# First feed-forward product of a hybrid decoder block as seven half-size products

## The chip, the cores and the metric

The kernel runs on one core of one Trainium2 chip. The metric is device time in microseconds (us) of one execution, the median of three runs. The engines that matter here are TensorE (PE in the profile, with its weight loads as PEld), VectorE (DVE), ScalarE (ACT), GpSimd (POOL) and SyncE (SP); SP, ACT and POOL can also issue transfers.

## The reference

One decoder layer on 512 tokens of width 1024, all float32. A gated mixer (a pooling branch and an attention branch) is added to x; then comes the feed-forward part, which is what the change is about; then a last norm.

```
x   = x + (gate_a * a + gate_b * bm) @ w_out
hm  = rmsnorm(x, g_mlp)
x   = x + square(relu(hm @ w_mlp_in)) @ w_mlp_out     # w_mlp_in 1024 x 4096, w_mlp_out 4096 x 1024
out = rmsnorm(x, g_final)
```

## The kernel before

**Precision.** Each matmul operand is split in two float32r parts, hi (a rounding copy on ScalarE, L62) and lo (the rest, a subtraction on VectorE, L63). A product is three matmuls: hi·hi, hi·lo and lo·hi (`mm3`, L67 to L69, for products with the weights as stationary operand; `rows_mm`, L762 to L764, for those with the rows as stationary operand).

**Weights.** `load_chunk` (L93) loads 512 KB of a weight matrix into a `raw` tile (four buffers), issued by SP, and `split` makes `whi` and `wlo` (four buffers each). The second feed-forward product's pairs (`pair_of`, L841) use the same four `whi`/`wlo` buffers.

**Stages.** In order: first norm, latents, pooling and the gate A product (to about 142 us), eight attention heads with the gate B product filling in (to 260 us), attention projection, `w_out` product with the second norm and its transposes (to 350 us), then the feed-forward part. Before the feed-forward loop an order written out by hand (`manual_schedule`) holds in the first stage and around the `w_out` product. Elsewhere a planner orders each engine's instructions ahead of time by priority and its own cost model, and may move a ready instruction ahead of one that is not.

**Feed-forward part.** The 4096 hidden columns are four groups (`q` = 0 to 3) of eight blocks of 128. For each block, `load_up` loads and splits 1024 x 128 of `w_mlp_in`, `up_mm` makes 24 matmuls (8 slices of the contraction, 3 passes) of 128 x 512 into one PSUM bank, and `up_end` (L854) applies relu and square on ScalarE. The first three blocks run as two token halves each (256 columns), because the last rows' norm is not done yet (L816 to L823). When both blocks of a pair are done, `up_end` forms the sums S1, S3, S2, S4 of the hidden values' quarters and splits seven forms of them into `rhi`/`rlo`.

`down(q)` (L908) then makes the second product of the group by seven products of half-size quarters (a Winograd form). Its weight sums are formed in SBUF by adding transfers that GpSimd issues (`plus`, L922) onto `X` tiles, of which there are six buffers. Each product takes 168 / 7 = 24 matmuls of 128 x 512, in two banks. Results are added by VectorE (L906) into the residual rows `xa` or into U, V5 and V7, which `flush` (L1029) adds up before the last group.

Of the kernel before, what the change touches and what calls it, by code (L numbers as in the profile page):

```python
# [11 lines left out]
F32 = mybir.dt.float32  # L12
F32R = mybir.dt.float32r
I32 = mybir.dt.int32
AF = mybir.ActivationFunctionType
# [26 lines left out]
NX = 6  # L42
# [3 lines left out]
def block_kernel(ctx: ExitStack, tc: tile.TileContext, x, positions, g_mix, w_in, b_gate,  # L46
# [46 lines left out]
    def load_chunk(srcs, cols, parts=False, own=None):  # L93
# [3 lines left out]
        raw = wp.tile([P, 1024], F32, name=f"raw{n}", tag="raw", bufs=4)  # L97
        hi = (own or wp).tile([P, 1024], F32R, name=f"whi{n}", tag="whi", bufs=3 if own else 4)
        lo = (own or wp).tile([P, 1024], F32R, name=f"wlo{n}", tag="wlo", bufs=3 if own else 4)
# [63 lines left out]
    gB = spill.tile([P, KD, S], F32, name="gB")  # L163

# [65 lines left out]
    with ExitStack() as pre:  # L230
# [334 lines left out]
        pool_in(1)  # L565
        latents_t(3)
        pool_diff(0)
        load_u(3)
        pool_in(2)
        pool_diff(1)  # L570
        load_a(0)
        split(praw, pw_hi, pw_lo)
        pool_in(3)
        q_rotary_w()
        load_a(1)
        gate_a(0)
        pool_diff(2)
# [3 lines left out]
        gate_a(1)  # L581
        pool_diff(3)
# [3 lines left out]
        gate_a(2)  # L586
        load_p(0)
# [5 lines left out]
        gate_a(3)  # L593
        pool_proj(0)
# [3 lines left out]
        gate_a(4)  # L598
        pool_proj(2)
        load_a(6)  # L600
        gate_a(5)
        pool_proj(3)
        load_p(2)
        load_a(7)
        gate_a(6)
        project_w(0)
# [13 lines left out]
    with ExitStack() as att:  # L620
# [82 lines left out]
        for h in range(NH):  # L703
            if h + 1 < NH:
                project_w(h + 1)
            scores(h, 0)
            scores(h, 1)
# [21 lines left out]
    m_hi = keep.tile([P, KD, S], F32R, name="m_hi")  # L729
    m_lo = keep.tile([P, KD, S], F32R, name="m_lo")  # L730
    g2 = keep.tile([P, D], F32, name="g2", tag="g")
# [35 lines left out]
    w1_v = w_mlp_in.rearrange("(k p) c -> p k c", p=P)  # L767
    w2_v = w_mlp_out.rearrange("(k p) c -> p k c", p=P)
    nc.sync.dma_start(g2, g_mlp.partition_broadcast(P))
    wp2 = pool(norm, "wp2")  # L770
    order = ExitStack()
    order.enter_context(tc.manual_schedule(engines=ENGINES))
    hrow, wo, up_w = {}, {}, {}
# [3 lines left out]


    NG = FF // P // FFG
    HALF = FFG // 2  # L780
    ff_order = [q * FFG + j + k * HALF for q in range(NG) for j in range(HALF) for k in range(2)]

    def load_up(ff, own=None):
        up_w[ff] = chunk(w1_v[:, :, ff * P:(ff + 1) * P], KD, P, own=own)

    for k2 in range(4):
        load_out(0, k2)
    for c in range(2):
        cs = slice(c * 512, (c + 1) * 512)
        for t in range(NT):  # L790
# [10 lines left out]
            if c == 1:  # L801
                if t:
                    transpose_rows(hrow[t - 1], t - 1, m_hi, m_lo, psT, "n2")
                hrow[t] = norm_rows(xa[:, t, :], t, g2, tmp, "n2")
                if t < 3:
                    load_up(ff_order[t], own=wp2)
# [5 lines left out]
    def up_mm(w, ps, tok):  # L812
        proj_t(ps[:, tok], w, m_hi[:, :, tok], m_lo[:, :, tok], 0, KD, KD)


    lo_t, hi_t = slice(0, 256), slice(256, 512)  # L816
    first = [(up_w.pop(f), psM.tile([P, S], F32, name=f"up{f}", tag="mm")) for f in ff_order[:3]]
    up_mm(*first[0], lo_t)
    up_mm(*first[1], lo_t)
    transpose_rows(hrow[3], 3, m_hi, m_lo, psT, "n2")  # L820
    up_mm(*first[2], lo_t)
    for f in range(3):
        up_mm(*first[f], hi_t)  # L823
# [12 lines left out]
    A21, A11, S3, S1, S2, S4, A22, A12 = range(8)  # L836
# [4 lines left out]
    def pair_of(raw):  # L841
# [5 lines left out]
        return [t.rearrange("p (a b) -> p a b", a=2) for t in (hi, lo)]  # L847

    U, V5, V7 = (fp.tile([P, 2, 512], F32, name=n) for n in ("U", "V5", "V7"))
    C = {(1, c): xa[:, 2:4, c * 512:(c + 1) * 512] for c in range(2)}  # L850
    C.update({(2, c): xa[:, 0:2, c * 512:(c + 1) * 512] for c in range(2)})
    forms, F_of = {}, {}

    def up_end(ff, ps):  # L854

        q, j, k = ff // FFG, ff % FFG % HALF, ff % FFG // HALF
        if k == 0:
            F_of[q, j] = fp.tile([P, 8, 256], F32, name=f"F{q}_{j}", tag="F", bufs=1)
# [17 lines left out]
    for n in range(3):  # L876
        up_end(ff_order[n], first[n][1])
# [201 lines left out]
```

## Time and profile before

| | before |
|---|---|
| median of three runs | 700.42 us (700.18 to 700.74) |
| the profiled execution | 699.11 us |
| its span, first to last instruction | 697.3 us |
| mean granted TensorE clock | 0.992 |
| VectorE, ScalarE, GpSimd busy | 433.5, 325.7, 82.3 us |
| transfers | 93.07 MB, 133 GB/s over the span |

Times below are microseconds from the start of the span. In the groups of instructions a row names line, engine, operation, tiles (out<-in) and shape, then the busy time in us and the mean duration in ns of one, then the engine's idle time just before them and who ended it. Matmul durations there overlap each other; the distance between two starts says what one costs.

### The profile page before, as it was taken

How to read it: one execution, taken by the hardware profiler on the slowest of the kernel's cores; microseconds unless marked ns; L12 is line 12 of the kernel's file. 1: busy time of each engine (PE TensorE's matmuls, PEld its weight loads, DVE VectorE, ACT ScalarE, POOL GpSimd, SP SyncE). 2: the span in 40 equal slices, each digit the busy share in tenths (PEclk: the TensorE clock that was granted, in tenths of full speed). 3: DMA queues.
4: the chain of work that ended last, by engine and by line, in shares of the span. 5: the costliest groups of instructions: out<-in, count | busy, mean ns of one | idle time of the engine just before them, and what ended most of it. 6: DMA issues, size and time to landing. Idle time of an engine off the chain costs nothing.

```text
span 697.3 us, 8522 instructions
## 1 busy us (share of the span) xinstructions
PE 681.9 (98%) x3177; PEld 558.8 (80%) x3177; DVE 433.5 (62%) x693; ACT 325.7 (47%) x509; POOL 82.3 (12%) x98
## 2 busy tenths in 40 slices
PE   6999999999999999999999999999999999999994
PEld 3988888888888888888898888887888888888883
DVE  5868642678878745534655556346764467945776
ACT  4545332556556445312534653455434553355534
POOL 2317400000000000000002021001210102101111
PEclk8999999999999999999999999999999999999998
DMA  7424343542301227644467679535994458903453
GB/s 269 137 62 126 92 150 110 164 120 68 101 23 50 88 89 245 183 134 132 125 181 239 137 167 230 163 71 112 185 238 119 92 120 205 244 3 60 97 85 121
DMA packets 101314, 93.07 MB, mean 133 GB/s; under 512 B 6404, under 2 KB 75800, under 8 KB 101272
## 3 DMA queue, kind: packets, MB, share of 16 engines
q1 hardware_dynamic: 92568, 75.74, 35.1%
q0 software_dynamic: 8704, 16.78, 14.9%
q8 instruction: 25, 0.41, 0.2%
q14 instruction: 17, 0.14, 0.1%
HBM read 86.22 MB, written 6.29 MB: 133 GB/s over the span
## 4 chain that ended last, share of the span: by engine, by line
PE 93%; DVE 2%; DMA 2%; ACT 1%; issue 1%; SPq 0%; POOL 0%; POOLq 0%; DVEq 0%; ACTq 0%
PE up L69 9%; PE up L67 9%; PE up L68 9%; PE P L763 7%; PE P L764 7%; PE P L762 7%; PE u L406 3%; PE lat L338 3%; PE wo L764 2%; PE ga L68 2%; PE wo L762 2%; PE ga L69 2%; PE wo L763 2%; PE ga L67 2%; PE bm L69 2%; PE bm L67 2%
## 5 line engine op out<-in xcount | busy, mean ns | idle before, releaser
L63 DVE TENSOR_TENSOR wlo<-raw,whi 128x1024 fp32r<-128x1024 f32 x73 | 89.4, 1230 | 64.2 <-ACT whi L62 58.7
L62 ACT CAST whi<-raw 128x1024 fp32r<-128x1024 f32 x73 | 75.9, 1050 | 101.5 <-PE up L68 32.8
L67 PE MATMUL up<-m_hi,whi 128*128 128x512 f32 (+1 forms) x280 | 105.5, 377 | 0.0
L69 PE MATMUL up<-m_hi,wlo 128*128 128x512 f32 (+1 forms) x280 | 105.3, 376 | 0.0
L68 PE MATMUL up<-m_lo,whi 128*128 128x512 f32 (+1 forms) x280 | 105.3, 376 | 0.0
L63 DVE TENSOR_TENSOR xlo<-X,xhi 128x1024 fp32r<-128x1024 f32 x56 | 68.3, 1223 | 50.3 <-ACT xhi L62 50.2
L62 ACT CAST xhi<-X 128x1024 fp32r<-128x1024 f32 x56 | 58.5, 1049 | 73.0 <-PE P L764 56.3
L763 PE MATMUL P<-xlo,rhi 128*128 128x512 f32 (+1 forms) x228 | 88.5, 391 | 0.0
L762 PE MATMUL P<-xhi,rhi 128*128 128x512 f32 (+1 forms) x228 | 88.5, 391 | 0.0
L764 PE MATMUL P<-xhi,rlo 128*128 128x512 f32 (+1 forms) x228 | 87.7, 391 | 0.0
L924 POOL DMA_DIRECT2D X<-in_w_mlp_out x32 | 38.4, 1205 | 276.4 <-DVE xlo L63 215.3
L68 PEld LDWEIGHTS up<-m_lo,whi 128*128 128x128 f32 x280 | 52.7, 188 | 10.5
L69 PEld LDWEIGHTS up<-m_hi,wlo 128*128 128x128 f32 x280 | 52.6, 188 | 10.5
L67 PEld LDWEIGHTS up<-m_hi,whi 128*128 128x128 f32 x280 | 52.6, 188 | 10.5
L762 PEld LDWEIGHTS P<-xhi,rhi 128*128 128x128 f32 x228 | 42.8, 188 | 10.5
L764 PEld LDWEIGHTS P<-xhi,rlo 128*128 128x128 f32 x228 | 42.7, 188 | 10.1
L763 PEld LDWEIGHTS P<-xlo,rhi 128*128 128x128 f32 x228 | 42.8, 188 | 9.9
L63 DVE TENSOR_TENSOR rlo<-F,rhi 128x1792 fp32r<-128x1792 f32 x16 | 32.4, 2026 | 21.7 <-ACT rhi L62 21.7
L62 ACT CAST rhi<-F 128x1792 fp32r<-128x1792 f32 x16 | 27.0, 1689 | 19.7 <-DVE F L870 19.7
L861 ACT ACTIVATE F<-up 128x512 f32<-128x512 f32 x32 | 18.9, 594 | 21.0 <-DVE rlo L63 13.5
L67 PE MATMUL gb<-h_hi,whi 128*128 128x512 f32 x64 | 26.4, 412 | 0.0
L650 ACT ACTIVATE p<-s,nm 128x128 f32<-128x128 f32 (+3 forms) x32 | 16.8, 527 | 19.7 <-DVE nm L647 19.0
(236 smaller groups left out, 1314.9 us busy)
## 6 DMA issues: line engine op xcount, KB each, us to landing
raw<-in_w_mlp_in SPq DMA_DIRECT2D x32, 512.0 KB, 4.9
X<-in_w_mlp_out SPq DMA_DIRECT2D x32, 512.0 KB, 5.0
X<-in_w_mlp_out POOLq DMA_DIRECT2D x32, 512.0 KB, 6.1
raw<-in_w_in SPq DMA_DIRECT2D x20, 512.0 KB, 3.9
raw<-in_w_attn_proj SPq DMA_DIRECT2D x8, 512.0 KB, 3.6
raw<-in_w_out SPq DMA_DIRECT2D x8, 512.0 KB, 4.1
x<-in_x SPq DMA_DIRECT2D x4, 512.0 KB, 8.4
raw<-in_w_pool_proj SPq DMA_DIRECT2D x4, 512.0 KB, 3.3
```

The costliest lines, as they stand in the source:

```text
L62: nc.scalar.copy(hi, src)
L63: (lo_eng or nc.vector).tensor_tensor(out=lo, in0=src, in1=f32(hi), op=ALU.subtract)
L67: nc.tensor.matmul(acc, whi, ahi, start=first, stop=False)
L68: nc.tensor.matmul(acc, whi, alo, start=False, stop=False)
L69: nc.tensor.matmul(acc, wlo, ahi, start=False, stop=last)
L338: nc.tensor.matmul(ps[:, :LAT], h[:, k, tok], w[:, k % 2, :], start=len(done) == 1, stop=len(done) == 3 * KD)
L406: nc.tensor.matmul(ps, w[:, k, :], a[:, k, :], start=n + k == 0, stop=n == 2 and k == KD - 1)
L762: nc.tensor.matmul(acc, a_hi, w_hi, start=first, stop=False, skip_group_check=again)
L763: nc.tensor.matmul(acc, a_hi, w_lo, start=False, stop=False, skip_group_check=again)
L764: nc.tensor.matmul(acc, a_lo, w_hi, start=False, stop=last, skip_group_check=again)
L861: nc.scalar.activation(a, ps, AF.Relu)
L924: nc.gpsimd.dma_start(X[name, h].rearrange("p (a b) -> p a b", a=2), B[src, h], accum_op=ALU.add)
```

## The change

**The first product.** Each group `q` is now done in two passes (`d` = 0, 1) of 2 x 256 hidden columns. The contraction (1024) is cut in halves, the hidden columns of a group in halves, and the tokens in halves. With B the quarters of the transposed normed rows, and A those of the weights, a pass `up(q, d)` makes seven products: A11·B11, S1·T1, S2·T2, A12·B21, S3·T3, S4·B22 and A22·T4. S1 to S4 are sums of weight quarters, T1 to T4 sums of row quarters. Each product is 24 matmuls of 256 columns into one PSUM bank (`up_mm`: 2 blocks, 4 slices, 3 passes). The partial sums are shared in PSUM: ScalarE copies a bank once its first product is in (b from a, c from b, v from c), and later products go on adding to the copy and to the original.

**The weight sums.** In DRAM, ten sums of 1 MB (S1, S3, S2, S4 for group 0, S1 and S3 for groups 1 to 3) are formed early: a copy of one quarter, issued by ScalarE, in the first stage (`sum_copies`), and later an adding transfer of another quarter, issued by GpSimd (`sum_adds`: two in the first stage, one in each attention head). S2 and S4 of groups 1 to 3 are formed in SBUF: once S1's `raw` tile has been split, an adding transfer of 512 KB turns it into S2, and after S2's split another turns it into S4.

**What goes with it.** The four row sums T1 to T4 are formed and split once, right after the second norm. The rows' transposes are kept in float32 as well (`mT`, a ScalarE copy of each). The six `X` buffers of the second product are now one `X` buffer and the four `raw` ones, shared with the weights of the first; A11 of groups 1 to 3 uses the `X` buffer too. V7 is gone: that product is added to two rows' quarters at once. `gf` (the last gain) is loaded before the last `down` and not ahead of the loop. The seven forms of the second product's input are made per pass, for two blocks at a time.

```
+    IN_DRAM = [(q, n) for q in range(NG) for n in ((1, 3, 2, 4) if q == 0 else (1, 3))]
+    sums = {(q, n): spill.tile([P, 4, HALF * P], F32, name=f"S{n}_{q}") for q, n in IN_DRAM}
+    def sum_copies():
+        for q, n in IN_DRAM:
+            nc.scalar.dma_start(sums[q, n], block(q, {1: "21", 3: "11", 2: "11", 4: "12"}[n]))
+            yield
+    def sum_adds():
+        for q, n in IN_DRAM:
+            src = block(q, "22") if n == 1 else block(q, "21") if n == 3 else sums[q, 1 if n == 2 else 2]
+            nc.gpsimd.dma_start(sums[q, n], src, accum_op=ALU.add, max_dma_last_dim=2048)
+            yield
...
         pool_in(0)
+        next(copies)
...
             scores(h, 0)
+            next(adds)
...
+    def load_form(q, d, name, own=None):
...
+        if n in sums or not n:
+            src = (sums[n] if n else block(q, name[1:]))[:, :, cols]
+            raw = fp.tile([P, 1024], F32, name=f"XA{q}_{d}", tag="X", bufs=1) if q and name == "A11" else None
...
+                raw, hi, lo = load_chunk([(v, src)], 1024, True, own=own)
+        else:
+            raw = chain[q, d]
+            nc.gpsimd.dma_start(v(raw), block(q, {"S2": "11", "S4": "12"}[name])[:, :, cols], accum_op=ALU.add)
...
+    def transpose_norm(t):
+        for half in range(2):
...
+            if name != "B12":
+                hi, lo = (v[:, :, t % 2 * P:(t % 2 + 1) * P] for v in M[name])
+                split(pt, hi, lo)
+            nc.scalar.copy(mT[:, ks, tok], pt)
...
+    def up_mm(q, d, name, form, acc, fresh=False):
+        whi, wlo = up_w.pop((q, d, name))
+        bhi, blo = M[form]
+        for j in range(2):
+            js = slice(j * P, (j + 1) * P)
+            for k in range(4):
+                for n, (w, b) in enumerate(((whi, bhi), (whi, blo), (wlo, bhi))):
+                    nc.tensor.matmul(acc[:, j, :], w[:, k, js], b[:, k, :], start=fresh and j + k + n == 0,
+                                     stop=j == 1 and k == 3 and n == 2, skip_group_check=not fresh)
+    def start_up(q, d, ps=psM, tag="mm"):
+        a = bank(f"a{q}_{d}", ps, tag)
+        up_mm(q, d, "A11", "B11", a, fresh=True)
+        b = bank(f"b{q}_{d}")
+        nc.scalar.copy(b, a)
+        return a, b
+    ab = [start_up(0, 0), start_up(0, 1)]
+    transpose_norm(3)
+    for d in range(2):
+        up_mm(0, d, "A12", "B21", ab[d][0])
...
+    nc.vector.tensor_sub(tf[0], B["B11"], B["B12"])
+    split(tf[0], *M["T1"])
+    nc.vector.scalar_tensor_tensor(out=tf[1], in0=tf[0], scalar=-1.0, in1=B["B22"], op0=ALU.mult, op1=ALU.subtract)
+    split(tf[1], *M["T2"])
...
+    def up(q, d):
...
+        need("S1")
+        e = bank(f"e{q}_{d}", psU, "up")
+        up_mm(q, d, "S1", "T1", e, fresh=True)
+        e_sb = F[:, S1]
+        nc.scalar.copy(e_sb, e)
+        need("S2")
+        up_mm(q, d, "S2", "T2", b)
+        c = bank(f"c{q}_{d}")
+        nc.scalar.copy(c, b)
+        if q:
+            need("A12")
+            up_mm(q, d, "A12", "B21", a)
+        relu2(A21, a)
+        need("S3")
+        up_mm(q, d, "S3", "T3", c)
+        v = bank(f"d{q}_{d}")
+        nc.scalar.copy(v, c)
+        need("S4")
+        up_mm(q, d, "S4", "B22", b)
+        nc.vector.tensor_add(F[:, A12], e_sb, c)
+        nc.vector.tensor_add(F[:, A11], e_sb, b)
+        relu2(A12, F[:, A12], -1.0)
+        relu2(A11, F[:, A11])
+        pairs(A11, A11 + 1)
+        need("A22")
+        up_mm(q, d, "A22", "T4", v)
+        relu2(A22, v, -1.0)
+        flat = F.rearrange("p f j c -> p f (j c)")
+        nc.vector.tensor_sub(flat[:, S1], flat[:, A21], flat[:, A22])
+        nc.vector.tensor_tensor(out=flat[:, S3:S2 + 1:2], in0=flat[:, 0:S1 + 1:3],
+                                in1=flat[:, A11].unsqueeze(1).to_broadcast([P, 2, 512]), op=ALU.subtract)
+        nc.vector.tensor_add(flat[:, S4], flat[:, A12], flat[:, S2])
+        pairs(S3, S2 + 1)
+        pairs(S4, S4 + 1)
+        pairs(A22, A12 + 1)
...
-                X[name, h] = fp.tile([P, 1024], F32, name=f"X{name}_{q}_{h}", tag="X", bufs=NX)
+                own = (name, h) == ("11", 0)
+                X[name, h] = (fp if own else wp).tile([P, 1024], F32, name=f"X{name}_{q}_{h}",
+                                                      tag="X" if own else "raw", bufs=1 if own else NRAW)
...
-        if last:
-            into(C[2, 1], p7)
-            into(C[2, 0], p7, ALU.subtract)
-        else:
-            set_or_add(V7, p7)
+        into(C[2, 1], p7)
+        into(C[2, 0], p7, ALU.subtract)
...
     for q in range(NG):
-        for ff in ff_order[max(q * FFG, 3):(q + 1) * FFG]:
-            load_up(ff)
-            ps = psU.tile([P, S], F32, name=f"up{ff}", tag="up")
-            up_mm(up_w.pop(ff), ps, slice(0, S))
-            up_end(ff, ps)
+        for d in range(2):
+            up(q, d)
```

More of the change, by code (lines that the diff above doesn't have):

```diff
@@ L827, in block_kernel @@
     psU = pool(ctx, "psU", bufs=2, space=bass.MemoryType.PSUM)
-    A21, A11, S3, S1, S2, S4, A22, A12 = range(8)
+    A11, S3, S1, S2, A22, A12 = range(1, 7)
+    A21 = S4 = 0
     rp = pool(ctx, "rp", side="right")
```

155 lines of the change are left out of this document (94 added, 61 removed).

## Prediction

> **What bounds the kernel now.** I read the page from the top: span, engines, slices, chain.
>
> ```profile
> span 697.3 us, 8522 instructions
> PE 681.9 (98%) x3177; PEld 558.8 (80%) x3177; DVE 433.5 (62%) x693; ACT 325.7 (47%) x509; POOL 82.3 (12%) x98
> PE   6999999999999999999999999999999999999994
> DMA  7424343542301227644467679535994458903453
> PE 93%; DVE 2%; DMA 2%; ACT 1%; issue 1%; SPq 0%; POOL 0%; POOLq 0%; DVEq 0%; ACTq 0%
> ```
>
> TensorE is busy in every slice but the first and the last, and 93% of the chain that ended last is its own work. So the kernel gets shorter by matmul time taken out, so long as nothing else makes TensorE wait. A busy share can hide a slow pace, so I looked at starts in the timeline of TensorE: first the two token halves of 256 columns that open the feed-forward part, then blocks of 512 columns.
>
> ```profile
> 350.30 0.28 PE L68 MATMUL up<-m_lo,whi 128*128 128x256 f32 x1
> ...
> 355.81 0.28 PE L69 MATMUL up<-m_hi,wlo 128*128 128x256 f32 x1
> ...
> 391.66 0.40 PE L68 MATMUL up<-m_lo,whi 128*128 128x512 f32 x1
> ...
> 396.09 0.40 PE L69 MATMUL up<-m_hi,wlo 128*128 128x512 f32 x1
> ```
>
> The first pair of rows is 46 starts apart: 5.51 / 46 = 0.1198 us for a matmul of 256 columns. The second is 19 apart: 4.43 / 19 = 0.2332 us for 512. Two halves cost 0.2396, 3% more than the whole. This is the price that decides here, and the kernel before shows it for exactly the shape, operands and bank that the change uses.
>
> **The change part by part.** *The matmuls.* The groups by shape give the count:
>
> ```profile
> L67 PE MATMUL up<-m_hi,whi 128*128 128x512 f32 x232 | 91.8, 396 | 0.0
> L67 PE MATMUL up<-m_hi,whi 128*128 128x256 f32 x48 | 13.7, 286 | 0.0
> ```
>
> Lines 67 to 69 each have these counts: 696 matmuls of 512 and 144 of 256, that is 696 x 0.2332 + 144 x 0.1198 = 162.3 + 17.3 = 179.6 us. After: 8 passes x 7 products x 24 = 1344 of 256 = 161.0 us. Removed: **18.6 us**. The Trainium skill ("TensorE: Matmul & The Clock Gate", section "Wait — 56ns, not 53.3ns?") gives the columns divided by 2.4 GHz and some 2.5 ns for a matmul; by it the saving would be 696 x 0.2158 + 144 x 0.1092 - 1344 x 0.1092 = 19.1 us. The rows above hold a larger fixed part, 0.1198 - (0.2332 - 0.1198) = 0.0064 us, so halving is dearer here than by the page.
>
> *The work beside it.* ScalarE and VectorE must now serve a pass of 7 x 24 x 0.1198 = 20.1 us.
>
> ```profile
> L63 DVE TENSOR_TENSOR wlo<-raw,whi 128x1024 fp32r<-128x1024 f32 x73 | 89.4, 1230 | 64.2 <-ACT whi L62 58.7
> L62 ACT CAST whi<-raw 128x1024 fp32r<-128x1024 f32 x73 | 75.9, 1050 | 101.5 <-PE up L68 32.8
> L63 DVE TENSOR_TENSOR rlo<-F,rhi 128x1792 fp32r<-128x1792 f32 x16 | 32.4, 2026 | 21.7 <-ACT rhi L62 21.7
> L62 ACT CAST rhi<-F 128x1792 fp32r<-128x1792 f32 x16 | 27.0, 1689 | 19.7 <-DVE F L870 19.7
> L861 ACT ACTIVATE F<-up 128x512 f32<-128x512 f32 x32 | 18.9, 594 | 21.0 <-DVE rlo L63 13.5
> L862 ACT ACTIVATE F<-F 128x512 f32<-128x512 f32 x32 | 20.0, 633 | 0.9
> L867 DVE TENSOR_TENSOR F<-F 128x512 f32<-128x512 f32 x16 | 11.1, 692 | 0.6
> L693 ACT COPY gbs<-gb 128x512 f32<-128x512 f32 x8 | 4.7, 585 | 0.0
> ```
>
> ScalarE per pass: seven weight casts of 1.05, four bank copies of 0.59 (b, c, v and e), four relus and four squares of 0.59 and 0.63, and the casts of 7 x 512 columns, twice 1.69: 7.4 + 2.3 + 4.9 + 3.4 = 18.0 us. Before, four blocks took 4 x (1.05 + 0.59 + 0.63) + 2 x 1.69 = 12.5 us of 22.4. VectorE per pass: seven wlo 8.6, four sums of 0.69 and one of 1.23 (both from rows above), twice 2.03: 16.7 us. So ScalarE goes from 56% to 89% of its stage, VectorE to 83%. Both still fit, so I take nothing for their sums; what it costs if they do not fit is a rival below.
>
> *The chain of adding transfers in SBUF.* In groups 1 to 3, S1's split must end before an adding transfer turns its tile into S2, and S2's split before it becomes S4.
>
> ```profile
> L924 POOL DMA_DIRECT2D X<-in_w_mlp_out x32 | 38.4, 1205 | 276.4 <-DVE xlo L63 215.3
> X<-in_w_mlp_out POOLq DMA_DIRECT2D x32, 512.0 KB, 6.1
> DMA to landing us min/median/max: 3.5/5.9/11.3
> ACT whi L62 <- PE up L68: 32.8, 10, 4.3
> ```
>
> The last row is a wait: casts already wait for the matmuls to free one of four whi buffers, so a split can begin at most three products (3 x 2.88 = 8.6 us) before its own product. Counted from S1's cast: split 1.05 + 1.23 = 2.3, issue 1.2 and landing 6.1 (an adding transfer of the same size), S2's split 2.3, together 11.9 us; in the written order S2's product is due at 8.6 + 2.9 = 11.5, so 0.4 late. From S2's split to S4's: 7.3 + 2.3 = 9.6 us, due three products later at 8.6: 1.0 late. That is 1.4 us a pass, 8.4 us in the six passes. But the planner may put A12 ahead of S2 and A22 ahead of S4, each 2.88 us of cover; and before the change the X tiles went through the same kind of chain while TensorE's slices stayed at 9. I take 0.5 us a pass, **3 us** in all; bounds are 0 and the written order with a landing of 11.3. The Trainium skill ("DMA: Bandwidth & Descriptors", section "Anatomy of one DMA — SWDGE (gpsimd) path") has 2.0 us plus the bytes over 436 GB/s for such a transfer, 3.2 us for 512 KB; by it the chain would cost nothing. The row above measures nearly twice that, so the row is used.
>
> *The turn into the feed-forward part.*
>
> ```profile
> 354.70 1.42 DVE L130 SCALAR_TENSOR_TENSOR n2h<-xa,n2r,g 128x512 f32<-128x512 f32 x2 [0.44 <-POOL n2r L87]
> 356.56 1.07 ACT L62 CAST m_hi<-n2pt 128x512 fp32r<-128x512 f32 x2 [2.64 <-PE n2pt L140]
> ```
>
> The last rows' norm ends at 356.1, just as two half-block products end on TensorE (355.9): no slack. ScalarE now has three instructions of about 0.6 between the transposes of row tile 2 and that norm instead of two: +0.6. After the last transposes TensorE has A12 twice (5.8 us). T1 needs a copy, a sum, a cast and a subtraction (0.6 + 1.23 + 1.05 + 1.23, with hand-offs 4.5), so it is in time; each later T takes 1.23 + 1.05 + 1.23 = 3.5 on a chain beside products of 2.88, while the weights' own wlo lie on VectorE between them. In group 0 S3 follows S2 with only the bank copy between, 0.6 and hand-offs, twice. Together I take **3 us** (bounds 0 and 8, the second if all of the last three T wait behind a wlo of 1.23 and each copy waits behind a cast).
>
> *From a pass to the second product.* After A22 come relu, square, S1, both S3 and S2, S4, a cast of three forms (1.45) and its subtraction (1.74): 0.59 + 0.63 + 0.69 + 1.23 + 0.69 + 1.45 + 1.74 = 7.0, with hand-offs 8. Product 1 needs only A11's form (5.6 us) and half of product 7 only the earlier pass (2.8): 8.4 us of cover, but X splits share both engines. Taken: 1 us a group, **4 us**; bounds 0 and 3 a group.
>
> *Transfers.*
>
> ```profile
> X<-in_w_mlp_out SPq DMA_DIRECT2D x32, 512.0 KB, 5.0
> q1 hardware_dynamic: 92568, 75.74, 35.1%
> q0 software_dynamic: 8704, 16.78, 14.9%
> 40.00:140.00 100.00, 100.00 (x443) 81.17 (x442) 59.28 (x94) 39.95 (x63) 24.43 (x28) 1.00 0.43 123
> 140.00:250.00 110.00, 109.81 (x608) 94.05 (x607) 86.49 (x215) 63.56 (x157) 3.34 (x14) 1.00 0.24 71
> 397.00:436.00 39.00, 39.00 (x169) 31.30 (x168) 25.05 (x26) 19.79 (x24) 7.15 (x6) 1.00 0.84 193
> ```
>
> Plain transfers moved 75.74 MB in 244.8 us of all engines, 309 GB/s; adding ones 16.78 MB in 103.9 us, 161 GB/s. A group of 1 to 3 now needs 18 plain ones of 0.52 MB (30.5 us) and 12 adding ones (39.0 us), 69.5 us in 2 x 20.1 + 39.2 (168 matmuls of 512) = 79.5 us: 87%. It was 16 plain and 8 adding, 27 + 26 = 53 us, in 8 x 5.6 + 39.2 = 84: 63%. In the first stages ten copies of 1.05 MB take 34 us at 309 GB/s and 65 at 161, beside 43 used of 100; eight of the adds, 52 us, lie beside 26 of 110. So the early ones fit unless a copy inside DRAM goes at the adding rate: 0 taken, up to 8 us. Their issue on ScalarE lies in a stage where it is busy 40 of 100. V7's removal adds two VectorE sums a group in a stage where that engine is busy 25 of 39, 0. With fewer X buffers, product 7's second weight tile waits for the raw tile of the second pass's S3; that is split at best 8.6 us ahead of S3's product and 20 us ahead of product 7, and load, add and split take 5.0 + 7.3 + 2.3 = 14.6: 0, with some 6 us in hand.
>
> *Sum.* The profiled execution took 699.1 us (697.3 of span). 699.1 - 18.6 + 3 + 3 + 4 = 690.5; the median of the runs lies 1.3 above that execution, so **692**.
>
> **The rivals.** *All hidden.* The planner covers chain and tails as it does now: 699.1 - 18.6 and 1 to 3 for the turn, with the 1.3: 683 to 685. For it speaks the PE row's unbroken 9s; against it, no slack at 356 and a longer tail.
>
> *The SBUF chain becomes the bound (the other side).* If TensorE keeps the written order, each pass loses 1.4 us and twice whatever the landing takes beyond 6.1. The gain left before it is 18.6 - 7 = 11.6, so it decides from 1.9 us a pass, a landing of 6.4. At 7.0 it is 3.2 a pass, 19 us: 699.1 - 18.6 + 7 + 19 + 1.3 = 708. The transfers' rise to 87% and the maximum of 11.3 speak for it, the planner's freedom against it.
>
> *ScalarE is the bound of the passes.* 18.0 us with 20% of waits between its instructions is 21.6 against 20.1: 12 us in eight passes instead of the chain's 3, so 701.
>
> *Early copies hold up weight loads.* Half to all of the 8 us above: 696 to 700.
>
> That the change doesn't do what it says can be left out: the seven calls of `up_mm` stand in the diff.
>
> **How the numbers follow.** Forecast, 692 (own range 686 to 698): 0.42. All hidden: 0.20. SBUF chain: 0.22. ScalarE: 0.10, of which 0.06 within 0.2% (1.4 us, about what a measurement of this kernel tells from no change). Early copies: 0.06. Faster: 0.42 + 0.20 + 0.06 and 0.02 of ScalarE's, 0.70; the same 0.06; slower 0.22 + 0.02 = 0.24. The range, 683 to 708, leaves out the lower part of all hidden and the upper part of the chain.
>
> **What would show it.** Right: matmul starts of the seven products 0.12 apart, 1344 of them; TensorE's idle time in the passes below 2 us each; ScalarE near 90% there; no idle before 350. Wrong by the chain: gaps ahead of S2 or S4 products whose casts wait for a transfer. Wrong by ScalarE: casts back to back while TensorE waits for whi. Wrong by transfers: gaps before 350, or DMA at 9 through the loop with landings over 7.

## The result and the profile after

The changed kernel takes 784.65 us (median of 4 runs, 781.26 to 787.13) against 700.37 of the kernel before: 1.1199 times as long, 95% interval 1.1151 to 1.1248. The forecast was 692 and faster. The profiled execution has a span of 785.4 us; 697.3 less the 18.6 of matmul time would have been 678.7, so 106.7 us of stalls have to be found.

From the page of the changed kernel: span, TensorE's busy row, TensorE, granted clock and DMA in 40 slices of 19.6 us, and the chain's shares.

```profile
span 785.4 us, 9777 instructions
PE 694.5 (88%) x3681; PEld 590.6 (75%) x3681; DVE 482.2 (61%) x737; ACT 370.2 (47%) x589; POOL 107.2 (14%) x120
PE   6999994449999999999898998888988889988895
PEclk8999997769999999999999999999998999989998
DMA  7368999974312126645336794666947579564872
DMA 16%; PE 8%; DVE 5%; ACT 5%; issue 4%; POOL 1%; POOLq 0%; ACTq 0%; DVEq 0%
```

TensorE has one hole at slices 7 to 9, where DMA stands at 9, 9 and 7 and the clock at 7, 7 and 6, and from slice 20 on it is below full in most slices. Its share of the chain fell from 93% to 8%. Two stretches, then: before the feed-forward part and in it. TensorE's first feed-forward matmul, and the stretch up to it and behind it, in the windows view of after and of before (columns: window, length, busy time of PE, PEld, DVE, ACT, POOL, granted clock, DMA share, GB/s):

```profile
392.75 0.56 PE L906 MATMUL a<-mb_hi,whi 128*128 128x256 f32 x1
```

```profile
40.00:392.40 352.40, 316.25 (x1501) 259.61 (x1500) 201.57 (x377) 145.92 (x278) 39.67 (x55) 0.95 0.59 164
392.40:760.00 367.60, 328.02 (x1959) 291.02 (x1958) 236.08 (x254) 193.12 (x247) 54.97 (x45) 0.94 0.68 161
```

```profile
40.00:350.10 310.10, 309.90 (x1499) 256.47 (x1497) 196.04 (x375) 142.83 (x273) 29.44 (x45) 1.00 0.39 116
350.10:672.00 321.90, 321.90 (x1457) 262.42 (x1455) 193.34 (x213) 152.42 (x172) 39.84 (x33) 1.00 0.62 148
```

Before the feed-forward part TensorE now idles 352.4 - 316.3 = 36 us, and in it 367.6 - 328.0 = 40 us. The mean clocks of 0.95 and 0.94 can't be charged to the busy time as they stand, because the clock column covers idle time too. Inside the hole it reads 0.50 without a single matmul (windows of after):

```profile
150.00:154.00 4.00, 0.00 (x0) 0.00 (x0) 0.00 (x0) 0.00 (x0) 0.00 (x0) 0.50 1.11 223
```

Summed over windows of 2 us, busy time times the share of the clock that was missing is 4 us before the feed-forward part and 20.5 in it. Before the change TensorE idled 0.2 in these two stretches and lost nothing. The four add up to 101 of the 106.7 wanted; where the other 6 lie isn't shown.

**The first stretch.** Where GpSimd issues the early adding transfers (timeline of after: start, length, engine, line):

```profile
76.23 1.37 POOL L191 DMA_DIRECT2D S<-in_w_mlp_in  x1 [4.00 <-DMA S<-in_w_mlp_in]
91.47 1.16 POOL L191 DMA_DIRECT2D S<-in_w_mlp_in  x1 [11.29 <-DMA S<-in_w_mlp_in]
94.63 2.85 POOL L191 DMA_DIRECT2D S<-in_w_mlp_in  x2
113.46 1.04 POOL L191 DMA_DIRECT2D S<-S  x1 [15.98 <-DMA S<-in_w_mlp_in]
114.39 1.62 POOL L191 DMA_DIRECT2D S<-in_w_mlp_in  x1
130.52 1.03 POOL L191 DMA_DIRECT2D S<-S  x1 [14.52 <-DMA S<-S]
131.32 3.78 POOL L191 DMA_DIRECT2D S<-in_w_mlp_in  x3
```

How long copies (ACTq) and adds (POOLq) take from issue to landing, from the page's DMA issues of after (tile, queue, count, KB each, median us):

```profile
S<-in_w_mlp_in ACTq DMA_DIRECT2D x10, 1024.0 KB, 6.7
S<-in_w_mlp_in POOLq DMA_DIRECT2D x8, 1024.0 KB, 20.7
```

The same stretch in the windows of after, and of before:

```profile
100.00:150.00 50.00, 35.51 (x149) 28.34 (x147) 6.94 (x8) 5.28 (x7) 7.12 (x8) 0.86 1.10 253
```

```profile
100.00:150.00 50.00, 49.80 (x230) 40.74 (x229) 24.33 (x39) 19.32 (x33) 0.00 (x0) 1.00 0.54 159
```

And TensorE's two longest gaps in the timeline of after (the bracket is the idle time ahead and who ended it):

```profile
134.27 0.80 PE L69 MATMUL pa<-mx_hi,wlo 128*128 128x512 f32 x1 [11.25 <-DVE wlo L63]
...
167.43 0.77 PE L67 MATMUL qps<-cq_hi,wh 128*128 128x512 f32 x1 [20.67 <-DVE ya L518]
```

All ten adds are issued by 135 us, eight of which are written into the attention heads: the planner moved those ahead. There they lie beside the ten copies, the DMA engines are full (1.10, packets overlapping), and an add lands after 20.7 us. Loads and stores of that stage are late too (a 256 KB store of `ya` lands after 14.1 us at the median, 2.2 before the change), and TensorE stands 11.25 and 20.67 us.

**The feed-forward part.** The first pass of group 1 in the timelines of ScalarE, GpSimd and TensorE of after:

```profile
473.03 1.04 ACT L62 CAST whi<-raw 128x1024 fp32r<-128x1024 f32 x1
483.21 1.04 ACT L62 CAST xhi<-raw 128x1024 fp32r<-128x1024 f32 x1 [9.14 <-DMA raw<-in_w_mlp_in]
484.17 1.99 ACT L62 CAST whi<-raw 128x1024 fp32r<-128x1024 f32 x2
486.06 0.58 ACT L917 COPY b<-a 128x512 f32<-128x512 f32 x1
...
494.18 1.04 ACT L62 CAST xhi<-raw 128x1024 fp32r<-128x1024 f32 x1 [7.03 <-DMA raw<-in_w_mlp_in]
...
496.08 0.58 ACT L997 COPY c<-b 128x512 f32<-128x512 f32 x1
...
477.01 1.30 POOL L837 DMA_DIRECT2D raw<-in_w_mlp_in  x1 [15.60 <-DVE wlo L63]
...
486.69 0.39 PE L906 MATMUL b<-t_hi,xhi 128*128 128x256 f32 x1 [3.66 <-ACT b L917]
...
496.71 0.39 PE L906 MATMUL c<-t_hi,whi 128*128 128x256 f32 x1 [2.56 <-ACT c L997]
```

The cast at 473.03 is S1's. From it, the adding transfer (issued at 477.01) and ScalarE's wait of 9.14 us lead to S2's cast at 483.21, 10.2 us later; from there to S4's at 494.18 it is 11.0. While ScalarE stands it casts nothing ahead: the next two weight tiles follow only at 484.17, and behind them the copy of bank a into b. TensorE has been idle for 3.66 us when S2's product starts at 486.69, that is since 483.03. S2's cast ends at 484.25, so the late sum itself accounts for 1.2 us of the gap, and the other 2.4 are the two casts and the copy. At S4 it is plainer: what waits there is S3's product, on bank c. By the program's order its weights were among the casts at 484.17, but the copy of b into c stands behind the cast of S4, a product that is not due yet. In the first passes of the three groups ScalarE stands 15 to 16 us at these two casts, in the second passes 4 to 5. In the view of waits of after (total, times, longest):

```profile
ACT xhi L62 <- DMA raw<-in_w_mlp_in: 60.8, 12, 9.1
...
PE c L906 <- ACT c L997: 17.1, 7, 3.9
...
PE b L906 <- ACT b L917: 11.4, 6, 3.7
```

**The clock.** Windows of 2 us across these two gaps in after:

```profile
486.00:488.00 2.00, 1.31 (x10) 1.31 (x11) 1.79 (x2) 1.15 (x3) 1.30 (x1) 0.95 0.00 0
488.00:490.00 2.00, 2.00 (x11) 2.00 (x11) 0.00 (x0) 0.00 (x0) 0.00 (x0) 0.50 0.85 93
490.00:492.00 2.00, 2.00 (x15) 2.00 (x14) 0.00 (x0) 0.00 (x0) 0.00 (x0) 0.69 1.17 238
...
498.00:500.00 2.00, 2.00 (x12) 2.00 (x11) 0.89 (x1) 0.76 (x2) 0.00 (x0) 0.51 0.97 318
500.00:502.00 2.00, 2.00 (x14) 2.00 (x13) 0.00 (x0) 1.05 (x2) 0.00 (x0) 0.63 0.85 295
```

After both gaps TensorE starts again at full clock, falls to half about 1 us later and stays there for more than 3 us: 2 x 0.50 + 2 x 0.31 = 1.6 us lost after a gap of 3.66, 2 x 0.49 + 2 x 0.37 = 1.7 after one of 2.56. In the same trace half clock also followed gaps of 1.82 and 2.00 us (ahead of 521.34 and 595.72). The length alone doesn't decide: behind gaps of 2.81 us in e6 (ahead of 566.79) and 2.94 in e9 (ahead of 647.74) the clock stayed at 1.00. The Trainium skill ("TensorE: Matmul & The Clock Gate", section "HAM oscillation — how this bites in real kernels") warns of idle gaps above some 3.4 us; here shorter ones were enough.

### The profile page after: what moved, and what is told of

Read it like the earlier page. It is cut to its first block, busy times and chain, and to the rows that moved or that the text cites. A ratio compares the mean times of both kernels' runs of the same rounds, so it can differ in the third digit from the quotient of the medians.

```text
span 785.4 us, 9777 instructions
## 1 busy us (share of the span) xinstructions
PE 694.5 (88%) x3681; PEld 590.6 (75%) x3681; DVE 482.2 (61%) x737; ACT 370.2 (47%) x589; POOL 107.2 (14%) x120
## 3 DMA queue, kind: packets, MB, share of 16 engines
q10 hardware_dynamic: 5280, 10.49, 3.6%
## 5 line engine op out<-in xcount | busy, mean ns | idle before, releaser
L63 DVE TENSOR_TENSOR wlo<-raw,whi 128x1024 fp32r<-128x1024 f32 x79 | 99.2, 1264 | 29.6 <-ACT whi L62 28.3
L806 PEld LDWEIGHTS P<-xlo,rhi 128*128 128x128 f32 x228 | 43.6, 191 | 11.4 <-DVE xlo L63 1.5
L63 DVE TENSOR_TENSOR rlo<-F,rhi 128x512 fp32r<-128x512 f32 (+2 forms) x32 | 34.3, 1087 | 24.6 <-ACT rhi L62 24.6
L63 DVE TENSOR_TENSOR xlo<-raw,xhi 128x1024 fp32r<-128x1024 f32 x12 | 14.7, 1223 | 45.6 <-ACT xhi L62 45.6
L62 ACT CAST xhi<-raw 128x1024 fp32r<-128x1024 f32 x12 | 12.6, 1047 | 60.8 <-DMA raw<-in_w_mlp_in 60.8
L906 PE MATMUL c<-t_hi,whi 128*128 128x256 f32 x64 | 23.2, 362 | 17.1 <-ACT c L997 17.1
L837 POOL DMA_DIRECT2D raw<-in_w_mlp_in x12 | 15.5, 1291 | 139.3 <-DVE wlo L63 94.7
L906 PEld LDWEIGHTS c<-t_hi,whi 128*128 128x128 f32 x64 | 16.4, 256 | 18.7 <-ACT c L997 18.7
L1053 DVE TENSOR_TENSOR xa<-xa,P 128x512 f32<-128x512 f32 x46 | 29.6, 680 | 0.9 <-PE P L807 0.8
L62 ACT CAST rhi<-F 128x512 fp32r<-128x512 f32 (+2 forms) x32 | 29.6, 936 | 1.2 <-DVE F L1019 1.1
L67 PE MATMUL qps<-cq_hi,wh 128*128 128x512 f32 x16 | 7.4, 461 | 20.7 <-DVE ya L518 20.7
## 6 DMA issues: line engine op xcount, KB each, us to landing
S<-in_w_mlp_in POOLq DMA_DIRECT2D x8, 1024.0 KB, 20.7
```

The costliest lines, as they stand in the source:

```text
L62: nc.scalar.copy(hi, src)
L63: (lo_eng or nc.vector).tensor_tensor(out=lo, in0=src, in1=f32(hi), op=ALU.subtract)
L67: nc.tensor.matmul(acc, whi, ahi, start=first, stop=False)
L806: nc.tensor.matmul(acc, a_hi, w_lo, start=False, stop=False, skip_group_check=again)
L837: nc.gpsimd.dma_start(v(raw), block(q, {"S2": "11", "S4": "12"}[name])[:, :, cols], accum_op=ALU.add)
L906: nc.tensor.matmul(acc[:, j, :], w[:, k, js], b[:, k, :], start=fresh and j + k + n == 0, stop=j == 1 and k == 3 and n == 2, skip_group_ch ...
```

## The experiments

The theories, in words, since the letters in the expectations belong to their own batch. **Adds moved ahead**: the first stretch is lost because the planner pulls the adds of the heads into the first stage. **ScalarE stands at casts**: in the passes ScalarE waits in its fixed order at a cast whose adding transfer is late, and the bank copies behind it hold up TensorE. Rivals: the copies in DRAM alone do the harm; the chain is simply too long for the cover of the products; ScalarE has too much work. The first four ran beside the kernel before at 700.75.

**e1: GpSimd's order held as written in the heads.** Nothing left out.

```
+        held = ExitStack()
+        held.enter_context(tc.manual_schedule(engines={mybir.EngineType.Pool}))
         for h in range(NH):
...
+        held.close()
```

> The change with GpSimd's order in the attention heads fixed as written, so that each of the eight later adds in DRAM is issued in its own head and not in the first stage. Theory A (the adds, pulled forward by the planner beside the copies, fill the transfer engines and starve the weight loads): the feed-forward part starts before 360 where it started at 391, and the time falls by some 35 to 44 us, to about 745. Rival A2 (the copies inside DRAM do it by themselves): the start stays over 370, the time over 765.

758.45 us, 26 less, where 35 to 44 were expected. Six of the eight adds are now issued in the heads, from 169 us on; the median landing in the row below falls from 20.7 to 9.1 us, and the hole is nearly gone (a row of e1's windows, and one of its DMA issues):

```profile
100.00:150.00 50.00, 46.15 (x199) 36.83 (x198) 18.85 (x25) 14.58 (x22) 1.01 (x1) 0.97 0.94 266
```

```profile
S<-in_w_mlp_in POOLq DMA_DIRECT2D x8, 1024.0 KB, 9.1
```

The first feed-forward matmul comes at 362.4 instead of 392.75: the place of the adds, not their number, made 30 of the 42 us. With all ten copies still in place, the rival that they alone do the harm falls.

**e2: no copies and adds in DRAM** (each sum is read as one plain quarter: what is left out is the sum).

```
-    sums = {(q, n): spill.tile([P, 4, HALF * P], F32, name=f"S{n}_{q}") for q, n in IN_DRAM}
+    sums = {(q, n): block(q, {1: "21", 3: "11", 2: "11", 4: "12"}[n]) for q, n in IN_DRAM}
...
-            nc.scalar.dma_start(sums[q, n], block(q, {1: "21", 3: "11", 2: "11", 4: "12"}[n]))
...
-            nc.gpsimd.dma_start(sums[q, n], src, accum_op=ALU.add, max_dma_last_dim=2048)
```

> The change with all copies and adds in DRAM left out; the sums are read as one plain quarter of the weights, so the values are not the reference's. Both A and A2: the first stages are as before the change, the feed-forward part starts at 350 to 354, the time is about 741. If it stays over 755, the delay ahead of the loop has another cause than transfers.

753.89; first feed-forward matmul at 356.0. The ten copies and ten adds cost 31 us as the change places them, of which e1 gets back 26 without dropping one. The feed-forward gaps stay. These and the next runs without a spread given are single ones.

**e3: S2 and S4 of groups 1 to 3 loaded plainly** (their sums left out), the early transfers kept.

```
-        if n in sums or not n:
-            src = (sums[n] if n else block(q, name[1:]))[:, :, cols]
+        if True:
+            src = (sums[n] if n in sums else block(q, {"S2": "11", "S4": "12"}[name] if n else name[1:]))[:, :, cols]
...
-            nc.gpsimd.dma_start(v(raw), block(q, {"S2": "11", "S4": "12"}[name])[:, :, cols], accum_op=ALU.add)
```

> The change with S2 and S4 of groups 1 to 3 loaded as a plain quarter and not made by adding transfers onto S1's tile (values not the reference's); the early copies and adds stay. Theory B (the casts of S2 and S4 stand first in ScalarE's order and wait for the adding transfer, and the bank copies stand behind them): the gaps ahead of b and c go, 27 us, and with them the half-speed stretches after them, some 12 us; the time is about 745. Rival B2 (shared buffers, or the sums of ScalarE and VectorE): the gaps stay, the time is over 770.

746.37: the chain in SBUF is worth 38 us. The feed-forward stretch idles 12 us instead of 40 and its clock is back at 0.98, with every cast and copy of ScalarE still there, so that engine's work alone is not the bound; the first stretch keeps its hole (windows of e3, split at its own first feed-forward matmul):

```profile
40.00:395.70 355.70, 318.34 (x1505) 261.47 (x1504) 200.37 (x377) 147.07 (x282) 39.70 (x55) 0.94 0.59 163
395.70:719.00 323.30, 311.52 (x1960) 278.54 (x1959) 236.23 (x255) 192.25 (x248) 39.59 (x33) 0.98 0.71 183
```

**e4: both edits, e2 and e3.**

> Both left out: no copies or adds in DRAM, no adding transfers for S2 and S4 (values not the reference's); the matmuls, casts, bank copies and loads of the seven products stay. Theories A and B together: about 699, and 690 if the turn and the tails cost what the prediction took. Rival B2: over 725.

704.80: 80 us less than the changed kernel; e2's 31 and e3's 38 make 69, and the other 11 come only when both are gone. What is striking is what is left: with every first-product sum left out the kernel is still 4 us slower than before, and 12.8 above 692. TensorE's waits in e4:

```profile
PE P L802 <- ACT rhi L62: 5.9, 3, 2.1
PE n2pt L846 <- DVE n2h L130: 4.2, 2, 3.7
```

The turn into the feed-forward part (n2pt) and the turn into the second product (P). The next two take one each, from e4.

**e5: the float32 copies of the transposes put behind the next norm** on ScalarE (e4's sums are left out here too).

```
-            nc.scalar.copy(mT[:, ks, tok], pt)
+            kept.append((mT[:, ks, tok], pt))
...
                 hrow[t] = norm_rows(xa[:, t, :], t, g2, tmp, "n2")
+                for dst, pt in kept:
+                    nc.scalar.copy(dst, pt)
```

> e4_neither with the float32 copies of the transposed rows put behind the next row tile's norm on ScalarE for the first three row tiles (values not the reference's, as in e4). Theory T (these copies stand ahead of the last norm and so open the gap at 354, after which TensorE runs at half clock): the gap of 3.66 us at the last transposes shrinks below 1.5, the granted clock stays at 1.00 there, and the time falls by 4 to 6 us, to about 699. Rival: the norm waits for something else (the weight casts), and gap and time stay.

**e6: the form S3 = A21 - A11 made and split ahead of the A22 product**, not behind it with S2 (e4's sums left out).

```
         pairs(A11, A11 + 1)
+        nc.vector.tensor_sub(flat[:, S3], flat[:, A21], flat[:, A11])
+        pairs(S3, S3 + 1)
         need("A22")
```

> e4_neither with the form S3 made and split ahead of the A22 product, since it needs only A21 and A11 (values not the reference's, as in e4). Theory F (the tail of forms behind A22 is longer than product 1 and half of product 7 cover): the gaps of about 2 us ahead of P go in three or four groups, with the slow stretch behind each, so 4 x (2 + 1.5) = 14 us at most, time 691 to 698. Rival (P waits for its weight pairs, not its forms): the gaps stay, time 703 to 707.

700.86 and 700.19: 4 and 4.6 less than e4. The kernel before took 698.77 beside them and 700.75 beside e4, so a difference of 4 is uncertain by some 2. e5 did what was expected: the gap of 3.66 us ahead of the last transposes is gone, and the first feed-forward matmul comes at 351.1 instead of 355.6. e6 did not: the waits ahead of P were to go and the time to come to 691 to 698 us, but the waits are as long as in e4 (waits of e6):

```profile
PE P L802 <- ACT rhi L62: 6.2, 3, 2.8
```

What fell is the time lost to the clock, 10 us in e4 and 5 in e6, summed as above: two of the three slow stretches behind P are missing, one of them behind a gap that had grown to 2.81 us. So part of e6's gain is luck. Put on top of e5 (e12 below), the same edit takes these waits from 8.9 us to 3.8.

**e7: e1, with S2 and S4 of groups 1 to 3 made by GpSimd in SBUF** out of tiles that are there anyway. Nothing left out.

```
-            nc.gpsimd.dma_start(v(raw), block(q, {"S2": "11", "S4": "12"}[name])[:, :, cols], accum_op=ALU.add)
+            nc.gpsimd.tensor_tensor(out=raw, in0=raw, in1=plain[q, d, {"S2": "A11", "S4": "A12"}[name]], op=ALU.add)
```

> e1_adds_held with S2 and S4 of groups 1 to 3 formed by GpSimd from tiles in SBUF (one addition of 128 x 1024 each, estimated at 2.9 us from its 128 x 896 of 2.56 us before) in place of an adding transfer of 1.3 + 6.2 us. Theory B: the chain is shorter by 4.5 us a link, the gaps ahead of b and c of groups 1 to 3 (27 us with the slow stretches some 40) nearly go; time 711 to 722. Rival B3 (GpSimd's additions and VectorE's subtractions hold each other up): VectorE's mean for a wlo rises over 1.4 us and the time stays over 735.

720.94, 37.5 less than e1; the same sums at the same places of the order, but 2.46 us after the split instead of a transfer. TensorE's waits for b fall from 16.1 us to 0.7, those for c from 13.4 to 2.8 (waits of e7):

```profile
PE c L911 <- ACT c L1002: 2.8, 4, 1.3
```

The price appears on VectorE. GpSimd's sums in e7 (groups of instructions: busy us, mean ns), then one of them and a subtraction for wlo that began beside it (timelines of e7):

```profile
L840 POOL TENSOR_TENSOR raw<-raw,XA 128x1024 f32<-128x1024 f32 x6 | 14.8, 2462 | 74.6 <-DVE wlo L63 74.6
```

```profile
538.67 2.38 POOL L840 TENSOR_TENSOR raw<-raw,raw 128x1024 f32<-128x1024 f32 x1 [2.42 <-DVE xlo L63]
539.11 3.03 DVE L63 TENSOR_TENSOR wlo<-raw,whi 128x1024 fp32r<-128x1024 f32 x1
```

The mean of the 79 subtractions rose from 1225 ns in e1 to 1293, but their median stayed at 1.22 us: the rise is three of them, one a group, that took 3.0 us. Each began 0.4 us into one of GpSimd's additions and ended 1.1 us behind it. The Trainium skill ("SBUF — State Buffer", section "Who interferes with whom") has a VectorE instruction with two SBUF inputs contend with a GpSimd one that reads SBUF; these three agree with that.

**e8: e7 with the edits of e5 and e6.** Nothing left out.

> e7_gpsimd_sums with both e5's and e6's edit, a whole version of the change with nothing left out. If A, B, T and F all hold and add up: 711 less 5 less 10, about 697, so level with the kernel before or a little faster. If the gaps refill each other: 705 to 715.

715.51 (712.42 to 716.82), 1.0223 times the kernel before, interval 1.019 to 1.0256. The two turns give 5.4 of the 8.6 they gave in e4; TensorE waits 11.4 us for b, up to 3.3 at a time, so the wait moved. The time is just above the 705 to 715 expected for that case.

**e9: e1 with A12 written ahead of S2 and A22 ahead of S4**, 2.88 us of cover each. Nothing left out.

```
         nc.scalar.copy(e_sb, e)
+        if q:
+            need("A12")
+            up_mm(q, d, "A12", "B21", a)
         need("S2")
```

> e1_adds_held with the written order of the products changed: A12 ahead of S2, and A22 ahead of S4, so that one more product of 2.9 us covers each adding transfer; nothing is left out. Theory B with the landing as the cause: most of the gaps ahead of b and c (27 us, 40 with the slow stretches) go, time 715 to 735. Rival B4 (ScalarE's order alone: its casts of S2 and S4 are planned for an earlier landing than the real one, so other work stands behind them whatever the order of the products): the gaps stay at over 15 us, time over 740.

744.62: 14 less than e1, and the gaps stay, as the rival of ScalarE's order had it (waits of e9):

```profile
PE a L909 <- ACT xhi L62: 14.4, 3, 6.5
...
PE a L909 <- ACT b L920: 12.5, 6, 4.5
```

TensorE still waits 12.5 us for b, now with A12's product: it adds onto bank a, which the copy must have read first, and the copy stands behind S2's cast. The 14.4 us are the same thing one pass on: the cast of the next pass's A11 stands behind S4's, which waits for its adding transfer. With the cover that the prediction hoped the planner would give, the kernel is 45 us slower than before; so the chain was not only a matter of due times.

**e10: S2 of groups 1 to 3 formed in DRAM as well**, so that a pass has one adding transfer into SBUF (S4) and not two; six copies stay in the first stage, seven go to GpSimd in the heads, held in order; with the edits of e5 and e6. Nothing left out.

```
-    IN_DRAM = [(q, n) for q in range(NG) for n in ((1, 3, 2, 4) if q == 0 else (1, 3))]
+    IN_DRAM = [(q, n) for q in range(NG) for n in ((1, 3, 2, 4) if q == 0 else (1, 3, 2))]
...
+            for later in ((1, 2), (2, 1), (2, 3), (2, 2), (3, 1), (3, 3), (3, 2))[h:h + 1]:
+                copy_sum(*later, nc.gpsimd)
...
-        if name == "S1" and q:
+        if name == "S2" and q:
             chain[q, d] = raw
```

> A whole version with nothing left out: S2 of groups 1 to 3 formed in DRAM too, so that only S4 needs an adding transfer in SBUF, one link and no chain; six copies in the first stage, the other seven issued by GpSimd in the heads between the adds, held in their heads; e5's and e6's edits. If A and B hold: the feed-forward part starts at 351 to 357 and takes about 345, time 697 to 703, level with the kernel before. If 13 MB of copies and 13 MB of adds do not fit beside the heads: start over 360, time over 708.

699.23 (697.97 to 702.19, 10 runs) against 699.38: ratio 1.000, interval 0.9985 to 1.0014. All of the change's work is done, and 85 us of its stalls are gone; the gain is not there either.

**e12: e4 with the edits of e5 and e6; e11: e12 without the adding transfer for X12** in the second product (B12 + B22, now left out too).

```
-        plus("12", "22")
```

> e4_neither with e5's and e6's edits together: the seven products with all weight sums for nothing (values not the reference's), the least that the change could reach with these buffers. If the two edits add up: 705 less 4 less 4.6, about 696; the forecast's 690 if the tails go as well.

> e12_free_sums (e4 with e5's and e6's edits) without the adding transfer that makes product 7's weights in the second product (values not the reference's). Theory F2 (what is left ahead of P is again ScalarE standing at a cast, of X12, which waits for its adding transfer since its tile came late from the shared raw buffers, with the last forms behind it): the gaps ahead of P go, 2 to 3 us in each of four groups with the slow stretch, time 8 to 14 us under e12_free_sums. Rival (the forms' own length): the same as e12_free_sums within 3 us.

694.32 and 685.19. Without that add no entry of TensorE's waits is above 2.4 us in total, and the waits ahead of P for `rhi` are gone.

699.1 - 18.6 + 1.3 = 681.8 was the prediction's time with no stall at all; e11 stands 3.4 above it. Laid end to end, from the changed kernel to that sum: 80 us for the weight sums in both stretches, 10.5 for the two turns together (e12), 9 for X12's add, 3.4 not placed.

**e13: e10 with X12's sum formed in DRAM**, by four more copies and adds on GpSimd's queue: two of each in the heads, two in groups 1 and 2. Nothing left out.

```
+    def x12_copy(q):
+        nc.gpsimd.dma_start(x12[q], w2_v[:, q * FFG:q * FFG + 4, 512:])
+    def x12_add(q):
+        nc.gpsimd.dma_start(x12[q], w2_v[:, q * FFG + 4:q * FFG + 8, 512:], accum_op=ALU.add, max_dma_last_dim=2048)
...
-        plus("12", "22")
```

> e10 with the second product's only sum (B12 + B22) formed in DRAM as well, so that no half-size product waits for an adding transfer into SBUF. Four more copies and four more adding transfers of 1 MB go to GpSimd's queue: two of each in the heads, the others in groups 1 and 2 of the feed-forward part, their order on GpSimd kept as written; the eight adding transfers into the X buffers go. Nothing is left out. Theory A (the tail's remaining gaps are ScalarE standing at X12's cast for a late adding transfer; e11, without that add, was 9 us under e12): about 690, 699.2 less 9, faster than the kernel before by 1%, gaps ahead of the P products below 1 us but for the last. Theory B (the transfers are the limit: the heads' DMA share is 0.88 from 224 to 300 us in e10, and the loop's 0.76 to 0.79; 34 to 45 us more of the engines' time in copies and adds delay the loads instead): 697 to 706, with the feed-forward start after 355 us or waits for in_w_mlp_in loads in the loop.

701.62 (12 runs), 1.003 times the kernel before, interval 1.0016 to 1.0045. The time is that of theory B, and the gaps of theory A did go. The P gaps are down to one of 1.6 us, and the feed-forward part from one matmul of group 0 (the one on bank e behind a wait of 1.06 us) to the end took 698.9 - 380.5 = 318.4 us against 324.2 in e10. But that matmul came 7.5 us later, since the heads had too much to move (windows of e13 from 224 to 300, e10's row of the same window, and TensorE's gap in e13's timeline):

```profile
224.00:300.00 76.00, 70.45 (x330) 57.36 (x330) 37.47 (x76) 31.21 (x63) 7.69 (x10) 0.96 0.93 219
```

```profile
224.00:300.00 76.00, 75.47 (x360) 61.86 (x359) 43.40 (x82) 35.71 (x67) 6.67 (x9) 1.00 0.88 218
```

```profile
289.05 0.79 PE L67 MATMUL bm<-o_hi,whi 128*128 128x512 f32 x1 [5.51 <-ACT whi L62]
```

**e14: e13 without X12 in the heads**: group 0 as in e10, the sums of groups 1 to 3 copied at the end of the group before and completed in their own.

```
+                if q and d:
+                    x12_add(q)
                 up(q, d)
...
             down(q)
+            if q < NG - 1:
+                x12_copy(q + 1)
```

> e13 with X12's sums taken out of the heads: group 0's second product has its adding transfer into the X buffers back, as in e10, and the sums of groups 1 to 3 are copied in DRAM at the end of the group before and completed by an adding transfer in the middle of their own group's first product. Nothing is left out. In e13 the wait for X12 went, which was worth 5.8 us (first matmul of group 0's third form to the end: 318.4 against 324.2 in e10), and the heads lost 7.5 us (that matmul at 380.49 against 372.98) with a 5.51 us gap at 289.05 for a load that came late. If the heads' loss comes from X12's four transfers there (theory A), it goes here: that matmul at 373 again and 319 to 321 us behind it, 694 to 696 in all, faster than the kernel before. If the heads' loss is something else, or if the loop at a DMA share near 0.85 cannot take six more transfers (theory B): 699 to 704.

700.23 (11 runs), ratio 1.0006, interval 0.9996 to 1.0017. The heads are as in e10 again (that matmul at 373.4), the P gaps stay away, and the same time is lost at c, behind the cast of S4, whose adding transfer now shares the engines with six transfers of 1 MB more (timeline of ScalarE in e14):

```profile
615.02 1.04 ACT L62 CAST xhi<-raw 128x1024 fp32r<-128x1024 f32 x1 [7.25 <-DMA raw<-in_w_mlp_in]
...
617.40 0.59 ACT L1020 COPY c<-b 128x512 f32<-128x512 f32 x1
```

The best three whole versions, e10, e13 and e14, differ in where they wait and end within 0.4% of each other and of the kernel before. None is faster. What stays open: whether another order of ScalarE, with the bank copies ahead of the casts that wait, would get the rest; whether deeper buffers for `raw` or `X` would let the adds start earlier in time wasn't tried either.

## Why the prediction was wrong, point by point

**The matmuls: right.** 256 columns cost what the kernel before showed (24 starts of S1's product at 480.03 to 482.75, 0.118 us apart), and the saving exists: e11, with the new products and no chains but those of the X tiles, takes 685.2, within 3.4 of the stall-free sum. With idle time and clock losses taken out of the spans, window by window, 679 us are left in the kernel before and 661 in e11.

**"So the early ones fit": the first step that failed, and a whole stretch.** The sum put "eight of the adds" beside 26 of 110 us in the heads, because they are written there. The section on the kernel before says that the planner may move a ready instruction ahead, and an adding transfer that waits only for its copy is ready early. Charged where they ran, ten copies (34 us or more) and ten adds (65) beside 43 used made 142 of 100 us, by the prediction's own figures: the hole could have been worked out. The doubt that it did name, copies at the adding rate, did not come true: they moved 10.49 MB in 3.6% of the 785.4 us, 371 GB/s. Upper bound given 8; paid 31 (e2), of which the order alone is 26 (e1).

**The chain in SBUF: taken at 3 us, measured at 38 (e3).** The times were nearly right: 9.6 us from S1's cast to S2's (2.3 + 1.2 + 6.1) and 9.6 from S2's to S4's; measured 10.2 and 11.0, with a median landing of 6.1 as taken. The step that failed is what was done with them: they were set against the due times of S2's and S4's own products, 0.4 and 1.0 late. ScalarE's 18.0 us of work a pass was counted, and its order was given nothing. But an engine that works in order and stands 9 + 7 us of a first pass of 20.1 has no time for 18.0, and the copies b and c, which TensorE needs first, stand behind the casts. e7 (the same sums, promptly, 37.5 us back) and e9 (more cover, the gaps stay) speak for that, and the timelines show it; a run with only the copies moved ahead of the casts is missing. The rival nearest to it, the SBUF chain as the bound, had the sign and the place, but its price came from a landing that rises to 7.0; another, ScalarE as the bound, had the engine, with waits of 20% of its work in place of 56% (60.8 / 6 = 10.1 a pass, of 18.0).

**Nothing for the clock.** A gap was priced at its length. Here gaps of 2.6 and 3.7 us cost 1.6 to 1.7 more at half clock, and some 25 of the 107 us are that (4 and 20.5). The kernel before has it at its start: a gap of 2.23 us ahead of 9.86, then 5 us at 0.50; its mean clock of 0.992 was there to be asked about.

**The two turns: right in size, in part in place.** 3 and 4 were taken; e5 and e6 gave back 4 and 4.6, and 10.5 together. But the copies ahead of the last norm, which e5 moved, had been priced at 0.6 of the 3, and made a gap of 3.66 us. And the waits ahead of P were mostly not the forms' own length: they stayed in e6 and went with X12's add (e11).

**Fewer X buffers at 0: wrong.** The "some 6 us in hand" were for product 7's second weight tile, whose add is X12's. e11 puts that add at 9 us, though in e11 and e12 no sum of the first product stands beside it. That the four shared `raw` buffers keep it from starting earlier is argued, not shown: e13 only shows that the wait goes when the sum is ready in DRAM.

**DMA share.** The forecast of 87% for a group's transfers was near what the feed-forward part of the whole versions uses (0.76 to 0.85 from 400 to 600 us in e13's and e14's windows); it should have been read as the reason why every added transfer is late for something, which is what e13 and e14 show.

## What to carry to other kernels

A transfer costs what it costs where the scheduler puts it, not where it is written: before counting it beside idle DMA time, ask what it waits for, and if that is early, either count it early or hold its engine's order. On an engine that works in order, price a late input not by the instruction that needs it but by the next instruction behind it that someone waits for. Where a change opens idle gaps of a few microseconds on TensorE, add to each what the clock may take afterwards, here some 1.6 us where it did: half as much again for gaps of 3 us, little for one of 20.

## What the runs showed of the hardware

TensorE fell to half clock behind idle gaps of 1.82 to 3.66 us and stayed there for more than 3 us, 1.6 to 1.7 us lost at the two that were worked out; behind gaps of 2.81 and 2.94 us in e6 and e9 it did not fall. An adding transfer of 1 MB inside DRAM landed after 20.7 us beside the copies (DMA share 1.10), 9.1 in e1 with six of the eight in the heads; copies of the same size took 6.2 to 7.0. Three of VectorE's subtractions took 3.0 us instead of 1.22 beside an addition on GpSimd (e7). Copies issued by ScalarE, adds by GpSimd and loads and stores by SyncE lay in three queues, and still a 256 KB store took 14.1 us in the changed kernel and 2.3 in e2, without the copies and adds; the Trainium skill ("DMA: Bandwidth & Descriptors", section "Issuing engines are not separate DMA queues") says that they share 16 engines, and the rows of the changed kernel and of e13 show the price: 11.25 and 20.67 us of TensorE in the first stage, 5.51 in the heads.
